# Hyena stage: a fourth weight unit is split ahead, in tiles of the common pool, from the stage's first unit on

## The chip, the cores and the metric

The program runs on one core of one Trainium2 chip. The metric is the device time of one execution in microseconds (us), lower is better; it is given as the median of several executions. TensorE (PE in the profile) multiplies matrices, VectorE (DVE) and ScalarE (ACT) do elementwise work, GpSimd (POOL) does a little of it, and SyncE (SP) issues the DMAs.

## The reference

The computation is a two-layer backbone over 256 latent tokens and 256 context tokens of width 1024. Layer 0 mixes tokens by differential attention, layer 1 by Hyena, a long convolution done through a discrete Fourier transform. Each layer is a stack of half-step SwiGLU, mixer, half-step SwiGLU, with modulation and LayerNorm around each. The change concerns only the Hyena mixer of layer 1, which runs on the latent tokens:

```
u = dwconv3(h @ w_in, conv_w) + conv_b          # w_in: 1024 x 3072
x0, x1, v = split(u, 3)
y = irfft(rfft(x1 * v, 2L) * rfft(filter, 2L))  # long convolution, both directions
return (x0 * (y + (x1 * v) * d_skip)) @ w_o     # w_o: 1024 x 1024
```

## The kernel before, in words

Everything is float32, and every matrix product is made of three float32r matmuls: the weight is split in a high part `wH` and a low part `wL`, the activations likewise, and the product of the two low parts is left out. So each weight must be loaded, rounded to its high part by ScalarE (line 238) and subtracted from the raw value by VectorE (line 239), before TensorE can use it.

**The weight stream.** The class `Stream` holds all weight units in the order of their use, each 128 x 2048 values (1 MB) in the Hyena stage. A unit is loaded by SyncE (line 259) into one of two `raw` buffers, and when there is room, it is split. Room means: fewer than `W_BUFS` = 3 units hold a pair of `wH`/`wL` tiles, or fewer than `extra` units hold tiles of the common pool. A unit split into `wH`/`wL` takes two pieces of 1024 columns; a unit split into the common pool takes four pieces of 512 columns, each with its own pair of tiles `xwH`/`xwL`. `spare(n)` sets `extra` and calls `pump()`, which loads and splits all that there is room for at that place of the program. `done(it)` gives a unit's room back and pumps again. When a split is issued, it is put `LATER` = 200 steps later in the scheduler's priority than its place in the program.

**The common pool.** `blk` has 49 tiles of 128 x 512 float32. Nearly all intermediate values live in it: activations, spectra, tables, products. A tile is taken when its first writer is scheduled and given back after its last reader. A scheduler that goes by priorities and a model of the times fixes the order of the instructions on each engine before the program runs; on the chip each engine works its own list in order.

**The Hyena stage.** It has three parts. First, twelve units of `w_in` (called u0 to u11 here) are multiplied by the function `ramp`: u0 to u7 give x1 and v, u8 to u11 give x0. Units u0 and u1 go in step for the first five of the eight steps over the width; from u2 on each unit is 48 matmuls, into the PSUM tile `pxv`. After unit n, `end(pp, n)` does the short convolution (`cv`, or `x0keep` from u8 on), the product x1*v (`pkeep`), and the transposes of the product of unit n-2 (`ptr`, then split into `pTh`/`pTl`). After units 6 and 10 (`SPECTRUM`), `end` also runs the forward transform of one half of the channels: 24 matmuls into `uf`, then in `product` 13 or 14 VectorE instructions that multiply by the filter's spectrum, ending at line 1364 or 1366. At unit 9 the tables of the inverse transform are loaded (line 1306) and split (`bih`/`bil`). Second, eight groups of twelve matmuls into `yt` do the inverse transform, and VectorE multiplies by x0 and splits the result (`oh`). Third, `Project` multiplies by the four units of `w_o` (who0 to who3).

In `ramp`, a unit's room is given back right after its matmuls, except after units 6 and 10. There the call of `done`, and with it the split that it issues, stands behind the last VectorE instruction of the spectrum's product on VectorE's list:

```
            if f in late:
                with tc.issue_after(end(pp, f).ins):
                    st.done(it)
            else:
                st.done(it)
                end(pp, f)
```

In the kernel before, `extra` is 0 from the feed-forward stages until the line `st.spare(1)` behind the second part (line 1423). So during the twelve units only three units are split or in use at a time: u0 to u2 are split when the stage begins, and the end of unit n lets unit n+3 be split. The end of u6, behind the spectrum's product, lets u9 be split; the end of u10 lets who1 be split. The unit who3 is the one that goes into the common pool, after the inverse transform's matmuls have been issued.

Of the kernel before, what the change touches and what calls it, by code (L numbers as in the profile page):

```python
# [310 lines left out]
def backbone(ctx, tc, A, out):  # L311
# [106 lines left out]
    st = Stream(nc, tc, rawp, rawap, wsp, blk, items, strict)  # L418
# [93 lines left out]
    def gemm(outs, X, nk, k0=0, k1=None):  # L512

        for k in range(k0, nk if k1 is None else k1):
            xh, xl = X[k]
            for o, w, opens in outs:
                h, lo = w(k)
                mm(o, h, xh, opens and k == 0, False)
                mm(o, h, xl, False, False)
                last = mm(o, lo, xh, False, k == nk - 1)  # L520
        return last
# [760 lines left out]
    def ramp(unit, gemm, X, end, n, late=(), first=2, ks=5):  # L1282


        grp = [unit() for _ in range(first)]
        gemm([o for g in grp for o in g[2]], X, KT, 0, ks)
        for f in range(n):
            if f < first:
                it, pp, outs = grp[f]
                gemm(outs, X, KT, ks)  # L1290
            else:
                it, pp, outs = unit()
                gemm(outs, X, KT)
# [6 lines that stand above are left out]
# [21 lines left out]
    def hyena(X, au):  # L1321
# [17 lines left out]
        def spectrum(dh):  # L1339
            pT = pTs.pop(dh)  # L1340
            U = {}
            for f in range(2):
                for ft in (f, 2 + f):
                    ps = bank("uf")
                    for tt in range(2):
                        c = slice(P * ft, P * ft + P)
                        h, lo = pT[tt]
                        mm(ps, au[tt][0][:, c], h, tt == 0, False)
                        mm(ps, au[tt][0][:, c], lo, False, False)
                        mm(ps, au[tt][1][:, c], h, False, tt == 1)  # L1350
                    U[ft] = ps
                last = product(f, dh, U[f], U[2 + f])
            return last
# [34 lines left out]
        def end(pp, n):  # L1388
# [15 lines left out]
            if n in SPECTRUM:  # L1404
                return spectrum(SPECTRUM.index(n))

        ramp(unit, gemm, [(x[:, :T], x[:, T:]) for x in X], end, 12, SPECTRUM)
        O = []
        for j in range(KT):
# [25 lines left out]
    norm = ffn("a", 1, X, lambda: (tables.extend(split_table(A["a_u"], "au")), spec_load(0)))  # L1435
    X = ln_apply(norm, ln_params(1, 0), 1, x256, R)
    norm = hyena(X, tables)
    X = ln_apply(norm, ln_params(1, 1), 1, x256, R)
    st.spare(0)
# [26 lines left out]
```

## Time and profile before

| | |
|---|---|
| median of 3 runs | 1352.83 us (1350.25 to 1353.7) |
| the profiled execution | 1354.76 us, span 1353.0 us |
| TensorE busy | 1305.6 us (96%) |
| VectorE busy | 1031.9 us (76%) |
| ScalarE busy | 666.5 us (49%) |
| mean granted TensorE clock | 0.975 |
| the Hyena stage's twelve units | from 1014.8 to 1107.6 us |

An execution outside the profile and the profiled one differ by about 2 us, of which the median run is the shorter. A row of the timeline gives the start in us, the duration, the engine, the line, the operation, what it writes and reads, and in brackets the idle time of that engine ahead of it with what ended it. Rows for PE show how long each matmul was in the array; matmuls overlap, so the distance from one start to the next is the rate. A row of the table by stretches gives for each engine the busy time in us and the number of instructions, then the granted TensorE clock as a share of full speed.

### The profile page before, as it was taken

To read this page: it belongs to the slowest core of one execution; us is meant where nothing else is said; L and a number is where in the kernel's file an instruction comes from. 1 tells how busy PE (TensorE), PEld (TensorE's weight loads), DVE (VectorE), ACT (ScalarE), POOL (GpSimd) and SP (SyncE) were. 2 spreads that over 40 slices of the span, in tenths; PEclk is the share of its full clock that TensorE was granted. 3 is DMA by queue.
4 is the path that set the end of the run, shared out by engine and by line. 5 is a ranking of instruction groups with operands and counts; after the bars stand their busy time and mean duration, and the time that the engine had idled before them with its cause. 6 is when DMAs were issued, how large, how long until landed. Compare 5 with 4: busy or idle time off the path is not lost.

```text
span 1353.0 us, 19211 instructions
## 1 busy us (share of the span) xinstructions
PE 1305.6 (96%) x7394; PEld 1126.5 (83%) x7394; DVE 1031.9 (76%) x1913; ACT 666.5 (49%) x1185; POOL 12.7 (1%) x12
## 2 busy tenths in 40 slices
PE   7999999999999999998999999999999899999997
PEld 5588888888888788887888888888889798888886
DVE  5699998889887777768767668766768889766664
ACT  3543222222223867656765446665446444755543
POOL 0000000000000000000000000000000110000000
PEclk8999999999998999998999998999999999999999
DMA  8777798888841212212554464554653435345452
GB/s 320 306 293 277 270 347 333 311 346 317 326 151 73 94 63 94 94 63 92 204 198 172 153 209 156 204 194 156 218 210 125 141 125 183 129 179 188 146 189 78
DMA packets 44386, 261.39 MB, mean 193 GB/s; under 512 B 4932, under 2 KB 6660, under 8 KB 19592
## 3 DMA queue, kind: packets, MB, share of 16 engines
q1 hardware_dynamic: 44296, 260.18, 52.9%
q8 instruction: 58, 0.95, 0.3%
q14 instruction: 32, 0.26, 0.1%
HBM read 257.01 MB, written 3.15 MB: 192 GB/s over the span
## 4 chain that ended last, share of the span: by engine, by line
PE 81%; DVE 9%; ACT 4%; DMA 3%; issue 1%; ACTq 0%; SPq 0%; DVEq 0%
PE pa L335 23%; PE pu L335 22%; PE py L335 19%; PE pxv L335 5%; DVE wL L239 3%; PE pv L335 2%; ACT wH L238 2%; DMA raw<-woa 1%; PE pka L335 1%; PE hsp L335 1%; PE pkb L335 1%; PE uf L335 1%; PE lnst L335 1%; PE po L335 1%; DMA raw<-wib 1%
## 5 line engine op out<-in xcount | busy, mean ns | idle before, releaser
L239 DVE TENSOR_TENSOR wL<-raw,wH 128x1024 fp32r<-128x1024 f32 (+1 forms) x356 | 387.9, 1108 | 121.2 <-ACT wH L238 118.9
L238 ACT CAST wH<-raw 128x1024 fp32r<-128x1024 f32 (+1 forms) x356 | 328.7, 955 | 207.0 <-PE py L335 94.4
L335 PE MATMUL pa<-xhl,wH 128*128 128x512 f32 x520 | 189.0, 400 | 5.6 <-DVE xhl L822 5.6
L335 PE MATMUL pu<-xhl,wH 128*128 128x512 f32 x520 | 188.3, 398 | 0.0
L335 PE MATMUL py<-g,wH 128*128 128x512 f32 (+1 forms) x594 | 185.8, 371 | 0.0
L491 DVE SCALAR_TENSOR_TENSOR rawa<-rawa,condb 128x1024 f32<-128x1024 f32 x128 | 151.6, 1219 | 5.9 <-DMA rawa<-adr 5.7
L335 PE MATMUL py<-g,wL 128*128 128x256 f32 x528 | 147.4, 279 | 0.0
L335 PE MATMUL pa<-xhl,wL 128*128 128x256 f32 x520 | 147.2, 283 | 0.0
L335 PE MATMUL pu<-xhl,wL 128*128 128x256 f32 x520 | 147.1, 283 | 0.0
L335 PEld LDWEIGHTS py<-g,wH 128*128 128x128 f32 x594 | 107.1, 188 | 20.5
L335 PEld LDWEIGHTS pa<-xhl,wH 128*128 128x128 f32 x520 | 99.0, 191 | 29.1 <-DVE xhl L822 4.2
L335 PEld LDWEIGHTS pu<-xhl,wH 128*128 128x128 f32 x520 | 98.9, 190 | 22.9
L335 PEld LDWEIGHTS pa<-xhl,wL 128*128 128x128 f32 x520 | 100.0, 192 | 0.1
L335 PEld LDWEIGHTS pu<-xhl,wL 128*128 128x128 f32 x520 | 99.7, 192 | 0.0
L335 PEld LDWEIGHTS py<-g,wL 128*128 128x128 f32 x528 | 99.6, 189 | 0.1
L852 ACT ACTIVATE sil<-pa 128x512 f32<-128x512 f32 x22 | 13.2, 599 | 146.9 <-PE pa L335 146.9
L335 PE MATMUL pxv<-xhl,wH 128*128 128x256 f32 x384 | 73.7, 293 | 1.1 <-ACT xhl L820 1.1
L335 PE MATMUL pa<-xh,wH 128*128 128x512 f32 x176 | 68.8, 391 | 0.0
L335 PE MATMUL pa<-xl,wH 128*128 128x512 f32 x176 | 68.6, 390 | 0.0
L335 PE MATMUL pu<-xh,wL 128*128 128x512 f32 x176 | 68.6, 390 | 0.0
L335 PE MATMUL pu<-xl,wH 128*128 128x512 f32 x176 | 68.5, 389 | 0.0
L335 PE MATMUL pa<-xh,wL 128*128 128x512 f32 x176 | 68.5, 389 | 0.0
(315 smaller groups left out, 2593.9 us busy)
## 6 DMA issues: line engine op xcount, KB each, us to landing
rawa<-adr SPq DMA_DIRECT2D x64, 1024.0 KB, 6.9
raw<-wia SPq DMA_DIRECT2D x44, 1024.0 KB, 4.8
raw<-wib SPq DMA_DIRECT2D x44, 1024.0 KB, 4.7
raw<-woa SPq DMA_DIRECT2D x32, 704.0 KB, 4.3
raw<-wob SPq DMA_DIRECT2D x32, 704.0 KB, 4.1
rawa<-adx SPq DMA_DIRECT2D x8, 1024.0 KB, 9.6
raw<-wqk SPq DMA_DIRECT2D x8, 1024.0 KB, 4.7
raw<-whv SPq DMA_DIRECT2D x8, 1024.0 KB, 4.8
```

Source lines behind the costliest of these rows:

```text
L238: nc.scalar.copy(h[:, d], it["raw"][:, s:e])
L239: nc.vector.tensor_tensor(lo[:, d], it["raw"][:, s:e], h[:, d].bitcast(F32), OP.subtract)
L335: return nc.tensor.matmul(o, l, r, start=start, stop=stop, skip_group_check=True)
L491: V.scalar_tensor_tensor(junk if q else w, w, 1.0, condb[:, q, :], OP.mult, OP.mult, accum_out=mod[i][:, q, 2 * u + h:2 * u + h + 1])
L852: S.activation(s, pa, AF.Silu)
```

## The change

One line is added in `hyena`, ahead of the call of `ramp`:

```
             if n in SPECTRUM:
                 return spectrum(SPECTRUM.index(n))
 
+        st.spare(1)
         ramp(unit, gemm, [(x[:, :T], x[:, T:]) for x in X], end, 12, SPECTRUM)
         O = []
         for j in range(KT):
```

From here on one more unit may be split, into tiles of the common pool. With u0, u1 and u2 in the three `wH`/`wL` slots, u3 goes into the pool at once. After that, the end of unit n lets unit n+4 be split, and it takes the kind of tiles that unit n had: u3, u7, u11 and who3 stand in the pool, all others in `wH`/`wL`. The end of u6 now lets u10 be split, the end of u10 lets who2 be split. The later `st.spare(1)` finds nothing left to do. No matmul, no transform and no load is added or taken away; three units (u3, u7, u11) are split in four pieces of 512 columns where there were two of 1024.

More of the change, by code (lines that the diff above doesn't have):

```diff
@@ L1405, in end @@
                 return spectrum(SPECTRUM.index(n))
+        st.spare(1)
         ramp(unit, gemm, [(x[:, :T], x[:, T:]) for x in X], end, 12, SPECTRUM)
```

## Prediction

> **What bounds the kernel now.** I read the page first. TensorE is busy nearly all the time, and the chain that ended last is mostly its matmuls, so only time in which TensorE waits or runs at a lower clock can be won.
>
> ```profile
> span 1353.0 us, 19211 instructions
> ...
> PE 1305.6 (96%) x7394; PEld 1126.5 (83%) x7394; DVE 1031.9 (76%) x1913; ACT 666.5 (49%) x1185; POOL 12.7 (1%) x12
> ...
> PE 81%; DVE 9%; ACT 4%; DMA 3%; issue 1%; ACTq 0%; SPq 0%; DVEq 0%
> ```
>
> The change acts on one stage, so the table by stretches comes next: from unit u7 to the second transform, in steps of 10 us.
>
> ```profile
> core 0: us, PE busy (x) PEld busy (x) DVE busy (x) ACT busy (x) POOL busy (x), PEclk, DMA share, GB/s
> 1060.00:1070.00 10.00, 10.00 (x70) 9.34 (x69) 6.29 (x13) 3.74 (x7) 0.00 (x0) 1.00 0.40 152
> 1070.00:1080.00 10.00, 6.78 (x55) 6.37 (x53) 8.50 (x16) 5.66 (x12) 6.53 (x4) 1.00 0.18 54
> 1080.00:1090.00 10.00, 7.29 (x40) 6.83 (x41) 7.62 (x14) 3.38 (x7) 0.00 (x0) 0.66 0.40 135
> 1090.00:1100.00 10.00, 10.00 (x73) 9.43 (x72) 8.42 (x13) 6.96 (x10) 0.00 (x0) 1.00 0.75 284
> ```
>
> There is one hole: between 1070 and 1090 TensorE is idle for 20 - 6.78 - 7.29 = 5.93 us, and its clock falls to 0.66. Who ends the waits is in PE's timeline, and the lengths of the work in the chain.
>
> ```profile
> 1075.55 0.38 PE L1383 MATMUL ptr<-ident,pkeep 128*128 128x128 f32 x2
> 1075.69 0.48 PE L335 MATMUL pxv<-xhl,wH 128*128 128x256 f32 x2
> 1078.85 0.38 PE L335 MATMUL pxv<-xhl,wL 128*128 128x256 f32 x1 [2.69 <-DVE wL L239]
> 1082.71 0.69 PE L1383 MATMUL ptr<-ident,pkeep 128*128 128x128 f32 x2 [3.24 <-DVE pkeep L1397]
> 1084.78 0.41 PE L335 MATMUL pxv<-xhl,wL 128*128 128x256 f32 x1
> ...
> 1107.45 0.28 PE L335 MATMUL yt<-bih,yh 128*128 128x256 f32 x1
> ```
> ```profile
> 1058.54 5.46 PE uf L335 x24
> ...
> 1101.86 5.75 PE pxv L335 x48
> ```
>
> At 1075.69 TensorE begins u9 and lacks its low part: the first half comes at 1078.85, the second lets the unit go on at 1084.78. From 1075.69 to the first `yt` matmul at 1107.45 are 31.76 us. The work in it is three units of 5.75 (u9, u10, u11) and one transform of 5.46, 22.7 us together. So **9.0 us are lost there**: 5.9 idle, the rest by the clock.
>
> Why u9 is late is on VectorE's and ScalarE's lists.
>
> ```profile
> 1056.87 1.21 DVE L239 TENSOR_TENSOR wL<-raw,wH 128x1024 fp32r<-128x1024 f32 x1
> ...
> 1062.60 0.48 DVE L1328 SCALAR_TENSOR_TENSOR cv<-pxv,vec,cv 128x255 f32<-128x255 f32 x1 [3.15 <-ACT cv L1327]
> ...
> 1066.44 0.68 DVE L1359 TENSOR_TENSOR yr<-uf,spec 128x512 f32<-128x512 f32 x1
> ...
> 1075.90 0.69 DVE L1364 TENSOR_TENSOR yi<-yi,yt 128x512 f32<-128x512 f32 x1
> ...
> 1076.71 2.09 DVE L239 TENSOR_TENSOR wL<-raw,wH 128x1024 fp32r<-128x1024 f32 x1
> ...
> 1082.24 0.42 DVE L1397 TENSOR_TENSOR pkeep<-cv 128x256 f32<-128x256 f32 x1
> ...
> 1083.17 1.22 DVE L239 TENSOR_TENSOR wL<-raw,wH 128x1024 fp32r<-128x1024 f32 x1
> 1084.51 1.22 DVE L239 TENSOR_TENSOR wL<-raw,wH 128x1024 fp32r<-128x1024 f32 x1
> 1086.44 1.22 DVE L239 TENSOR_TENSOR wL<-raw,wH 128x1024 fp32r<-128x1024 f32 x1
> 1090.27 2.36 DVE L239 TENSOR_TENSOR wL<-raw,wH 128x1024 fp32r<-128x1024 f32 x2 [2.61 <-ACT wH L238]
> ```
> ```profile
> 1060.11 2.00 ACT L238 CAST wH<-raw 128x1024 fp32r<-128x1024 f32 x2 [2.56 <-DMA raw<-wh]
> ```
>
> ScalarE makes u9's high part at 1060.11, but its low part stands on VectorE behind the spectrum's product (1066.44 to 1076.59), as `ramp` orders for the unit that u6 makes room for. The four single pieces from 1076.71 on are u9's halves, then u10's; the pair at 1090.27 is u11.
>
> **The change part by part.** *u9 leaves the place behind the product.* It is now let in by the end of u5. Half a unit's high part takes 1.0 us and its low part 1.2, and VectorE had 3.15 us idle ahead of 1062.60. Its load had landed by 1060.11 (the wait ahead of that row is for it) and now can only come earlier, and u5's slot is free long before. So u9 is split before the product and TensorE runs it from 1075.69 to 1081.44. This removes the whole wait at u9; price on VectorE nothing, since 2.4 us fall in its 3.15 us gap. Without that cover the product would begin up to 2.4 us later.
>
> *u10 takes its place.* Now u10 stands behind the product. I let its halves take u9's old places: the first ends at 1078.80, the second at 1084.39. The first half is there when TensorE arrives at 1081.44; the second isn't, and since the two halves of a unit are used in turn at each step, TensorE waits until 1084.39: 2.95 us. The transposes of `pkeep` from 1082.24 lie within that wait. At best, the halves follow each other and end at 1079.9; then only the transposes wait, for about 1.2 us from 1081.44 to 1082.67. At worst, VectorE isn't a bit faster and the second half stays where u10's was, ending at 1087.66: 6.2 us.
>
> *The clock.* The stretches of 3.4 us around this hole and around another one show how the clock reacts:
>
> ```profile
> 582.40:585.80 3.40, 1.72 (x13) 1.32 (x13) 3.40 (x12) 2.82 (x6) 0.00 (x0) 1.00 0.55 234
> 585.80:589.20 3.40, 3.40 (x18) 3.40 (x17) 3.40 (x8) 2.81 (x7) 0.00 (x0) 0.50 0.02 5
> ...
> 1077.30:1080.80 3.50, 0.62 (x3) 0.41 (x3) 3.46 (x7) 1.88 (x5) 2.64 (x2) 0.99 0.00 0
> 1080.80:1084.20 3.40, 1.49 (x5) 1.27 (x6) 3.40 (x7) 1.00 (x3) 0.00 (x0) 0.50 0.00 0
> 1084.20:1087.60 3.40, 3.40 (x16) 3.16 (x16) 3.40 (x6) 0.78 (x2) 0.00 (x0) 0.50 0.59 207
> ```
>
> After a stretch with TensorE half idle (1.72 of 3.40 us busy) the next one has half the clock and 1.7 us of it are lost. At the present hole two stretches are slow, in which 1.49 + 3.40 us of matmuls run at half rate: 2.4 us lost. A wait of 2.95 us should still cost one slow stretch, 1.7 us. The Trainium skill (TensorE: Matmul & The Clock Gate, The HAM clock gate) says that the clock falls after at least one idle window of about 3.4 us. By that rule the new wait would leave the clock alone and the gain would be 1.7 us larger; the rows at 582.40 speak against it, where half a window was enough.
>
> *Sum at the matmuls.* The loss of 9.0 us becomes 2.95 + 1.7 = 4.65 us: **4.35 us gained**. With the second half at its best place it becomes 1.2 us, a gain of 7.8; with the worst one 6.2 + 2.4, a gain of 0.4.
>
> *The four-piece splits.* u3, u7 and u11 are split in four pieces:
>
> ```profile
> L238 ACT CAST xwH<-raw x8: 603/612/622, 1126.3 to 1164.9; 128x512 fp32r<-128x512 f32 x8
> L239 DVE TENSOR_TENSOR xwL<-raw,xwH x8: 678/692/693, 1126.9 to 1166.2; 128x512 fp32r<-128x512 f32 x8
> ```
> ```profile
> L239 DVE TENSOR_TENSOR wL<-raw,wH x14: 1207/1218/2114, 1054.7 to 1124.2; 128x1024 fp32r<-128x1024 f32 x14
> ```
>
> Four times 0.692 is 2.77 us on VectorE against 2.44, and 2.45 on ScalarE against about 2.1: 0.35 us more on each, three times. For u3 and u7 it is hidden, since from u1 to u7 TensorE doesn't wait; the first and the last of these stretches, all four full:
>
> ```profile
> 1020.00:1030.00 10.00, 10.00 (x86) 10.00 (x85) 7.99 (x17) 8.07 (x14) 0.00 (x0) 1.00 0.25 85
> ...
> 1050.00:1060.00 10.00, 10.00 (x80) 9.71 (x79) 8.97 (x17) 4.17 (x8) 0.00 (x0) 1.00 0.72 263
> ```
>
> u11's is behind u10's and ahead of its use by about 2 us or more (VectorE reaches it by about 1088, TensorE at about 1097). If uncovered it costs 0.35.
>
> *The DMAs.* No load is added; all come earlier. u11's load now follows u9's split instead of waiting for it until 1084.4, so the 2.61 us that VectorE waited for u11 go. SP's list also holds the loads of the second spectrum and of the tables; they stay between the same units, and the tables are needed only at 1107.
>
> *What is late next.* Behind the matmuls stands VectorE's work for the second product and for `oh`:
>
> ```profile
> 1098.73 0.68 DVE L1359 TENSOR_TENSOR yr<-uf,spec 128x512 f32<-128x512 f32 x1
> ...
> 1107.60 0.69 DVE L1364 TENSOR_TENSOR yi<-yi,yt 128x512 f32<-128x512 f32 x1
> ...
> 1125.36 0.41 DVE L510 TENSOR_TENSOR oh<-pkeep,oh 128x256 fp32r<-128x256 f32 x1
> ```
>
> It must move forward by the same 4.35 us, or the gain is lost at `oh`. Ahead of it VectorE has u9's pieces less (2.09 + 1.22 = 3.3), 0.35 more for u11, and 2.61 of idle time less to wait for: room for 5.6 us. who1's split moves ahead of the second product, who2 takes its place behind it. So I count nothing lost here, and nothing gained. Later stages see the same stream, with who3 in the pool in both kernels.
>
> So the profiled execution's 1354.76 us (span 1353.0 and 1.76 around it) would become 1350.4, and the median of 1352.83, which lies 1.9 below the profiled one, **1348.5**.
>
> **The rivals.** *The hole closes (gain 6 to 8, 1345 to 1347).* VectorE puts u10's halves close together, or the clock stays up. For it: with u9 gone, `pkeep` and u10 are all that is urgent behind the product. Against it: 1076.71 to 1084.39 also holds the convolutions of u7 and u8, which the order before put between the two halves. By the skill's rule on the clock, above, the time would be 1352.8 - 6.05 = 1346.8.
>
> *The gain is eaten on VectorE (gain 0 to 2, about 1352).* u10's halves stay where they are, or u11's pieces are put ahead of them. The same list of VectorE work then ends at the same time and TensorE only waits at u10 instead of u9. By the bound above the gain is 0.4. Against it: 3.3 us of work really leave the stretch.
>
> *The pool runs out (slower).* The place is u11's split. Counted from the code, at about 1092 the pool holds 43 of its 49 tiles: 4 of the residual, 8 inputs, 4 tables and 4 transposes of the forward transform, 4 `pkeep`, 5 of the spectrum, 8 products, 4 tables of the inverse, 2 `x0keep`. u11's eight make 51. Two low pieces would have to wait until the second transform's last matmul gives back eight tiles. If VectorE takes them up at once, that costs about 1.4 us. If they come behind the second product, which runs from 1098.73 to 1108.29, 9.6 us, of which 3.1 lie ahead of the transform's end at 1101.86, TensorE waits 6.4 + 1.4 = 7.8 us at u11 and 2.4 for the clock: 10.2, so 1352.8 - 4.35 + 10.2 = 1358.7. It decides the sign as soon as more than 4.35 us of that product stand ahead of the last piece. Against it: the split's place in the priorities, 200 steps behind u7, is just ahead of that product.
>
> *It does nothing* would need that the room isn't used; but u3 is loaded at that time and goes in at once, so I give it no chance of its own.
>
> **How the numbers follow.** I give the main case 0.55, with a range of its own from 1346.8 to 1350.3; the closed hole 0.18; the gain eaten 0.15; the pool 0.12. A measurement of this kernel tells about 0.3% (4.1 us) from no change, so faster means below 1348.8. The main case lies across that line, a little more than half below it: 0.32 faster, 0.23 same. With the closed hole, faster is 0.50; with the eaten gain, same is 0.38; slower 0.12. The range from 1344.5 to 1354.0 takes in the first three cases and leaves out most of the pool's.
>
> **What would show it.** Right: no wait for `wL` at u9; one shorter wait for u10's second half near 1081 to 1084; the first `yt` matmul near 1103; xwH and xwL counted 34 where there are 22 now; u9's low part ahead of 1066. Wrong: TensorE's hole as long as before but at u10 (eaten); a wait for xwL ahead of u11, behind line 1364 or 1366 (pool); `oh` still ending near 1125 with TensorE waiting for it; or a new wait between 1025 and 1069, where there was none.

## The result, and the profile after

The changed kernel takes 1364.75 us in the median of five executions (1360.75 to 1367.79), the kernel before 1353.65 (1350.25 to 1355.59) beside it. A sixth execution, disturbed at 7244 us, is left out; with it the median is 1365.01, the figure that later expectations go by. The ratio on record is 1.0097, with a 95% interval from 1.0075 to 1.0118; the two medians differ by 0.8%, and a repetition (e16) gives 1.0100. So the change makes the kernel **slower by about 1%**, 11 to 12 us, outside the predicted range of 1344.5 to 1354.0. The profiled execution took 1364.75 us, with a span of 1363.0 against 1353.0.

On the first page nearly nothing changes: TensorE's busy time, the shares of the chain.

```profile
span 1363.0 us, 19224 instructions
...
PE 1308.0 (96%) x7394; PEld 1128.2 (83%) x7394; DVE 1034.0 (76%) x1919; ACT 667.0 (49%) x1191; POOL 13.3 (1%) x12
...
PE 81%; DVE 9%; ACT 4%; DMA 3%; issue 2%; POOL 0%; POOLq 0%; ACTq 0%; SPq 0%; DVEq 0%
```

The stage must be read in stretches, with the columns of the table shown of before.

```profile
1050.00:1060.00 10.00, 7.11 (x47) 7.12 (x48) 8.96 (x17) 4.45 (x9) 0.00 (x0) 0.83 0.73 274
...
1080.00:1090.00 10.00, 6.11 (x44) 5.90 (x44) 9.76 (x19) 6.67 (x12) 0.03 (x1) 0.90 0.66 236
1090.00:1100.00 10.00, 10.00 (x62) 9.20 (x61) 3.31 (x5) 3.39 (x5) 0.00 (x0) 0.93 0.66 238
...
1110.00:1120.00 10.00, 7.26 (x54) 6.46 (x54) 9.71 (x14) 4.55 (x9) 4.78 (x3) 1.00 0.01 2
1120.00:1130.00 10.00, 5.39 (x34) 5.19 (x33) 9.85 (x23) 2.33 (x7) 0.00 (x0) 0.78 0.51 197
```

Where before had one hole in TensorE's row, there are now three: 2.89 us idle in 1050 to 1060, 3.89 in 1080 to 1090, 2.74 + 4.61 = 7.35 in 1110 to 1130. And VectorE works only 3.31 us in the stretch from 1090, where in before it worked 8.42. What TensorE waited for in the whole stage:

```profile
PE ptr L1383 <- DVE pkeep L1397: 6.9, 2, 3.9
PE py L335 <- DVE oh L510: 4.6, 1, 4.6
PE yt L335 <- POOL yl L1370: 2.1, 2, 1.5
```

The wait for `wL` at u9 is gone, as predicted. In its place stand two waits for a `pkeep`, and at the end one for `oh`.

```profile
1052.89 0.44 PE L1383 MATMUL ptr<-ident,pkeep 128*128 128x128 f32 x2 [3.03 <-DVE pkeep L1397]
...
1087.83 0.53 PE L1383 MATMUL ptr<-ident,pkeep 128*128 128x128 f32 x2 [3.89 <-DVE pkeep L1397]
```

To compare runs, each point of the stage is counted from its first matmul of u0 (1014.78 in before, 1012.67 in after; all rows are TensorE's starts):

| us after the stage's start | before | after |
|---|---|---|
| first transform | 43.5 | 47.9 |
| inverse transform (`yt`) | 92.7 | 93.9 |
| Projection (`py`) | 104.2 | 109.2 |
| next stage (`pa`) | 136.9 | 148.0 |

The stage is 11.15 us longer, which is the whole loss: 1.24 up to `yt`, where 4.35 had been forecast as a gain, 3.79 from there to `py`, 6.12 in the Projection. Each run has one profile. The profile of e16, the same changed kernel, has 94.0, 109.3 and 150.1 us in the last three rows, so a difference of about 2 us between the stages of two profiles shows nothing.

The first two holes are read on VectorE's list.

```profile
1045.70 2.50 DVE L239 TENSOR_TENSOR xwL<-raw,xwH 128x512 fp32r<-128x512 f32 x4 [0.34 <-ACT xwH L238]
1048.12 0.87 DVE L1328 SCALAR_TENSOR_TENSOR cv<-pxv,vec,cv 128x255 f32<-128x255 f32 x2
1048.90 0.86 DVE L1329 SCALAR_TENSOR_TENSOR cv<-pxv,vec,cv 128x255 f32<-128x255 f32 x2
1049.68 1.21 DVE L239 TENSOR_TENSOR wL<-raw,wH 128x1024 fp32r<-128x1024 f32 x1
...
1052.41 0.75 DVE L1397 TENSOR_TENSOR pkeep<-cv 128x256 f32<-128x256 f32 x2
...
1076.55 4.56 DVE L239 TENSOR_TENSOR wL<-raw,wH 128x1024 fp32r<-128x1024 f32 x2
...
1081.23 1.28 DVE L239 TENSOR_TENSOR xwL<-raw,xwH 128x512 fp32r<-128x512 f32 x2
...
1082.64 1.28 DVE L239 TENSOR_TENSOR xwL<-raw,xwH 128x512 fp32r<-128x512 f32 x2
1083.84 0.47 DVE L1328 SCALAR_TENSOR_TENSOR cv<-pxv,vec,cv 128x255 f32<-128x255 f32 x1
...
1087.36 0.42 DVE L1397 TENSOR_TENSOR pkeep<-cv 128x256 f32<-128x256 f32 x1
1087.69 1.22 DVE L239 TENSOR_TENSOR wL<-raw,wH 128x1024 fp32r<-128x1024 f32 x1
...
1092.10 1.22 DVE L239 TENSOR_TENSOR wL<-raw,wH 128x1024 fp32r<-128x1024 f32 x1
1100.77 0.69 DVE L510 TENSOR_TENSOR bil<-tabf,bih 128x512 fp32r<-128x512 f32 x1 [7.46 <-ACT bih L509]
...
1102.95 0.68 DVE L1359 TENSOR_TENSOR yr<-uf,spec 128x512 f32<-128x512 f32 x1
```

u7's four pieces stand ahead of the convolutions of u3 and u4, a half of u8's between them and the `pkeep` that TensorE's transposes wait for: the first hole. In before u7's first half stood behind u3's `pkeep`:

```profile
1049.54 0.41 DVE L1397 TENSOR_TENSOR pkeep<-cv 128x256 f32<-128x256 f32 x1
...
1050.46 1.21 DVE L239 TENSOR_TENSOR wL<-raw,wH 128x1024 fp32r<-128x1024 f32 x1
```

u10's and u11's pieces stand ahead of u7's convolution: the second hole. Then comes the sight that matters most: at 1092.10 + 1.22 VectorE stops for **7.46 us**, for the second half of a table of the inverse transform (`bih`), and the second product, which stands behind it on the list, begins at 1102.95 in place of 1098.73 (90.3 us after the stage's start in place of 84.0). On ScalarE and SyncE that table looks so:

```profile
1100.12 0.62 ACT L509 CAST bih<-tabf 128x512 fp32r<-128x512 f32 x1 [2.69 <-PE uf L335]
```
```profile
1081.17 3.10 SPq L259 DMA_DIRECT2D raw<-who  x2
1084.33 0.43 SPq L1306 DMA_DIRECT2D tabf<-b_i  x1
1090.32 3.35 SPq L259 DMA_DIRECT2D raw<-who  x2
1093.72 0.42 SPq L1306 DMA_DIRECT2D tabf<-b_i  x1
```

ScalarE has the release of its output tile from a matmul of the second transform, so the pool was full: this wait, of 2.69 us, is the one that ended last. Ahead of the cast on ScalarE's list stands a pair of who's high parts, done at 1097.4. And the table's second load is issued only at 1093.72, behind four loads of the Projection's weights. In before both table loads were issued from 1070.27 on, ahead of all of those, and VectorE didn't stop ahead of the second half:

```profile
1070.27 4.53 SPq L1306 DMA_DIRECT2D tabf<-b_i  x2
...
1087.69 34.14 SPq L259 DMA_DIRECT2D raw<-who  x4
```
```profile
1085.85 0.68 DVE L510 TENSOR_TENSOR bil<-tabf,bih 128x512 fp32r<-128x512 f32 x1
```

### The profile page after: what moved, and what is told of

It is laid out like the page before. It is cut to its first block, busy times and chain, and to the rows that moved or that the text cites. A ratio compares the mean times of both kernels' runs of the same rounds, so it can differ in the third digit from the quotient of the medians.

```text
span 1363.0 us, 19224 instructions
## 1 busy us (share of the span) xinstructions
PE 1308.0 (96%) x7394; PEld 1128.2 (83%) x7394; DVE 1034.0 (76%) x1919; ACT 667.0 (49%) x1191; POOL 13.3 (1%) x12
## 4 chain that ended last, share of the span: by engine, by line
PE 81%; DVE 9%; ACT 4%; DMA 3%; issue 2%; POOL 0%; POOLq 0%; ACTq 0%; SPq 0%; DVEq 0%
PE pa L335 23%; PE pu L335 22%; PE py L335 20%; PE pxv L335 4%; DVE wL L239 3%; PE pv L335 2%; DMA raw<-woa 2%; ACT wH L238 1%; PE hsp L335 1%; PE pka L335 1%; PE pkb L335 1%; PE uf L335 1%; PE lnst L335 1%; PE po L335 1%; PE sc L1061 1%
## 5 line engine op out<-in xcount | busy, mean ns | idle before, releaser
L239 DVE TENSOR_TENSOR wL<-raw,wH 128x1024 fp32r<-128x1024 f32 (+1 forms) x350 | 381.4, 1108 | 115.2 <-ACT wH L238 113.0
L238 ACT CAST wH<-raw 128x1024 fp32r<-128x1024 f32 (+1 forms) x350 | 322.5, 954 | 210.8 <-PE py L335 98.3
L335 PE MATMUL pu<-xh,wH 128*128 128x512 f32 x176 | 68.5, 389 | 0.0
```

The costliest lines, as they stand in the source:

```text
L238: nc.scalar.copy(h[:, d], it["raw"][:, s:e])
L239: nc.vector.tensor_tensor(lo[:, d], it["raw"][:, s:e], h[:, d].bitcast(F32), OP.subtract)
L335: return nc.tensor.matmul(o, l, r, start=start, stop=stop, skip_group_check=True)
```

## The experiments

Three theories stood against each other. **P**: the pool is full, so `bih` waits for a tile. **Q**: the order of the lists; splits stand ahead of convolutions whose `pkeep` TensorE needs. **R**: in the Projection, who3's pieces stand ahead of `oh`. A fourth, **S** (the place of the table's load on SyncE's list), was added after e5. "Stage" is the time from u0's first matmul to the next stage's first. Each ratio is to runs of the kernel before on the same chip; times of different chips are best compared by these ratios.

**e1, the tables asked for later** (the changed kernel):

```diff
-TABLE_LOAD = 9
+TABLE_LOAD = 11
```

> The changed kernel with the inverse transform's tables loaded and split after unit u11 instead of after u9 (TABLE_LOAD 11). Theory P (the pool is full: u11's eight tiles leave no tile for the table's high part bih, which waits for the second forward transform, and VectorE stands 7.5 us behind it): the 7.5 us of idle time on VectorE ahead of bil go, the second product begins right behind the second transform, and the time falls by about 4 to 8 us from 1365, to 1357 to 1361; not the whole, since the tables' own load and split now come later. Theory Q (the loss is the order of the lists: splits stand ahead of the convolutions, and TensorE waits for pkeep): the two waits for pkeep of 3.0 and 3.9 us stay, and the time stays within 2 us of 1365.

1368.94 us, ratio 1.0124 (1.0097 to 1.0152): not faster. VectorE's idle time ahead of the second product went, and that product ran from 84.7 us after the stage's start, as in before (84.0). But on SyncE's list the table's loads now stood behind the next stage's weights, and TensorE waited for the table itself:

```profile
PE yt L335 <- ACT bih L509: 14.5, 1, 14.5
```

So the miss says nothing against P. It is the first sign that a load's place on SyncE's list counts.

**e2, u11 not in the pool** (the changed kernel; the room is taken back at the end of u6, so u3 and u7 alone stand in the pool):

```diff
+            if n == 6:
+                st.spare(0)
             if n == SPEC_LOAD:
```

> The changed kernel with the room taken back after u6's transform (spare(0) in end(6)), so that u3 and u7 are split into the pool, u11 is not, and from u11 on the stream is that of before. Theory P: the pool never fills, VectorE's idle time of 7.5 us and the late second product go, and the time comes back to 1353 or less (1347 to 1354). Theory Q: the wait for pkeep near 1052 of 3.0 us and its slow clock stay, the second one shrinks since u11's pieces no longer stand ahead of the convolution of u7; 1358 to 1362.

1350.16 us, ratio 0.9978 (0.9961 to 0.9996), 1.2% less than the change by the ratios. So the whole loss goes when u11 stays out of the pool. This run doesn't tell how: it relieves the pool, and it also gives u11 and the Projection's weights their old places, so that the table's second load stands behind one of them in place of four (issued 69.4 us after the stage's start) and the second hole shrinks to 1.1 us. The first hole is still there:

```profile
1056.96 0.44 PE L1383 MATMUL ptr<-ident,pkeep 128*128 128x128 f32 x2 [3.26 <-DVE pkeep L1399]
```

**e3, the kernel before with eight tiles of the pool held** from the stage's start to u11's end; eight small writes and reads are added:

```diff
+        held = [blk("held") for _ in range(8)]
+        for t in held:
+            V.memset(t[:, 0:8], 0.0)
...
+            if n == 11:
+                for t in held:
+                    nc.gpsimd.tensor_tensor(t[:, 0:8], t[:, 0:8], X0[5][:, 0:8], OP.add)
```

> The kernel before with eight tiles of the pool taken at the start of the Hyena stage and given back only after the convolution of u10; the stream and its splits are those of before. Eight tiny instructions on VectorE and eight on GpSimd are added for it. Theory P: the pool fills as in the changed kernel, bih waits for the second transform, VectorE idles some 5 to 8 us there, and the time is 6 to 11 us over before: 1359 to 1364. Theory Q: nothing is ahead of the convolutions, so the time stays within 2 us of 1353.5.

1356.87 us, ratio 1.0035 (1.0018 to 1.0053). Nothing of the weight stream is changed here, and yet VectorE stops ahead of `bil`:

```profile
1097.31 0.69 DVE L510 TENSOR_TENSOR bil<-tabf,bih 128x512 fp32r<-128x512 f32 x1 [6.66 <-ACT bih L509]
```

A full pool alone makes that stop. As in the change, ScalarE's list has a pair of who's high parts ahead of `bih` (done at 1094.4), and the last 2.25 us are for the tile, released by a matmul of the second transform. It costs about 4.5 us (2.4 to 7.2 by the interval), less than the 6 to 11 that P expected.

**e4, the kernel before with u9's split no longer behind the product:**

```diff
-        ramp(unit, gemm, [(x[:, :T], x[:, T:]) for x in X], end, 12, SPECTRUM)
+        ramp(unit, gemm, [(x[:, :T], x[:, T:]) for x in X], end, 12, SPECTRUM[1:])
```

> The kernel before without the order that puts the split after u6 behind the first product (only the one after u10 stays). If the hole at u9 is made by that order, as the prediction had it: u9 and u10 are split ahead of the product, TensorE's hole of 9.0 us shrinks to 1 to 3 us, and the time falls by 5 to 9 us to 1344 to 1349. If the hole is made by the load on VectorE as a whole (the same work has to be done before pkeep of u7): TensorE waits for pkeep instead, and the time stays within 3 us of 1353.5.

1355.88 us, ratio 1.0025 (1.0008 to 1.0043): no gain, though u9 was early and the wait for `wL` gone. The next unit's halves stood ahead of the product, and the first waited for a slot that u7 still held, and TensorE waited 3.8 and 4.4 us for what lay behind:

```profile
1070.25 1.22 DVE L239 TENSOR_TENSOR wL<-raw,wH 128x1024 fp32r<-128x1024 f32 x1 [6.06 <-ACT wH L238]
```

**e5, e6, e7: more tiles, and its controls.** A pool of 53 fits if the attention's weights have two raw buffers in place of three. e5 is the changed kernel with both, e6 the changed kernel and e7 the one before with two raw buffers alone.

```diff
-RAWA_BUFS = 3
-BLK_BUFS = 49
+RAWA_BUFS = 2
+BLK_BUFS = 53
```

> The changed kernel with 53 tiles in the common pool in place of 49; the room comes from the attention weights' raw buffers, two in place of three. In the stage the engines' lists are the same as in the changed kernel with two raw buffers and 49 tiles (e6), so that only the number of tiles differs. Count at the fullest point by the lists: 51 tiles. Theory P (pool full): VectorE's idle 7.46 us ahead of bil goes to under 1 us, the second product begins at 93 to 96 us after the stage's start in place of 90.3 to 104, the stage (first unit's matmul to the next stage's first) falls by 6 to 9 us against e6 and the total by as much. Theory Q (the splits' place in the lists is the whole loss): the stage falls by under 2 us, since the lists are the same. By either the two waits of TensorE's transposes for pkeep (3.0 and 3.9 us) and py's wait for oh (4.6 us) stay, so that the stage stays 3 to 6 us longer than the one of before.

> Control: the changed kernel with two raw buffers for attention weights and the pool of 49. All theories: the stage as in the changed kernel (135 us, within 2), the idle 7.5 us ahead of bil there; the total moves only by what the attention and the other stages lose to the missing buffer, 0 to 8 us.

> Control: the kernel before with two raw buffers for attention weights and the pool of 49. All theories: the stage as before (122 us, within 2); the total moves by the same 0 to 8 us as in e6, so that e6 less e7 is 11 to 13 us, as after less before.

| | time, us | ratio | stage, us |
|---|---|---|---|
| e7, before, 49 tiles | 1364.13 | 1.0100 (1.0074 to 1.0125) | 136.1 |
| e6, after, 49 tiles | 1377.01 | 1.0190 (1.0161 to 1.0220) | 149.8 |
| e5, after, 53 tiles | 1376.23 | 1.0181 (1.0151 to 1.0211) | 150.1 |

The missing buffer costs about 13 us in both (by the ratios), more than the 8 expected, and e6 less e7 is 12.9, about the change's own loss. The expectations put the stage at 135 and 122 us; by the measure used here it is 148.0 us in the change and 136.9 in before, and the controls lie within 2 us of that. But **P as put falls**: with four tiles more, nothing is won. In e5 the wait has another end:

```profile
1114.44 0.62 ACT L509 CAST bih<-tabf 128x512 fp32r<-128x512 f32 x1 [1.62 <-DMA tabf<-b_i]
```

The table's second load was issued at 1109.12, again behind four loads of the Projection. In both runs the cast of `bih`'s second half begins about 88 us after the stage's start (87.8 in e6, 88.5 in e5), held once by the tile and once by the load. Two causes end at nearly the same time, and taking one away shows nothing.

**e8, one unit in the pool for a short while** (the kernel before, with `st.spare(1)` at the end of u4 and `st.spare(0)` at that of u5):

> The kernel before, with room for one more unit in the pool only from the end of unit 4 to the end of unit 5: u8 alone is split into pool tiles, u3, u7 and u11 keep their slots. By the lists u9's split then stands ahead of u4's convolution and u10's behind the product. Theory P alone (nothing but the full pool cost time): the prediction's gain at the matmuls comes, 2 to 4 us, 1348 to 1351. Theory Q (a split put into the list ahead of a convolution holds the pkeep that a transpose waits for): the wait for wL at u9 goes and one for pkeep comes in its place in front of u5 to u7, 2 to 4 us; the total within 2 us of before, 1351 to 1355.

1351.81 us, ratio 1.0005 (0.9986 to 1.0025). The wait for `wL` is gone and one of 4.4 us for a `pkeep` has come, as Q expects.

```profile
1065.35 0.69 PE L1383 MATMUL ptr<-ident,pkeep 128*128 128x128 f32 x2 [4.42 <-DVE pkeep L1401]
```

**e9 and e10: the table's loads on a queue of their own**, with 49 and with 53 tiles (two raw buffers as in e5 to e7):

```diff
-            nc.sync.dma_start(t, src[:, 512 * h:512 * h + 512])
+            (nc.gpsimd if name == "bi" else nc.sync).dma_start(t, src[:, 512 * h:512 * h + 512])
```

> The changed kernel as in e6 (two raw buffers, 49 tiles), the inverse table's two loads issued from GpSimd's queue in place of SyncE's, where the second stands behind four loads of the Projection's weights. Only the queue is relieved; the pool is still full. Theory P (the full pool is what ends the wait, e5's 53 tiles having run into the table's load only 1.3 us short of it): bih's second cast still waits for the second transform, bil's idle 5 to 8.6 us on VectorE, total within 4 us of e6. Theory S (the load's place on SyncE's list is the whole cause): bil's idle under 1 us, total 6 to 9 us less than e6.

> The same with 53 tiles: queue and pool both relieved. Theory PS (two causes that end within 1.5 us of each other, so that taking away one alone, as in e5, brings nothing): bil's idle under 1 us, the second product begins at 91 to 96 us after the stage's start, the stage falls by 6 to 9 us against e5 and e6 and the total with it, 1367 to 1371, 3 to 7 above e7. Theory P as first put (e5 should have cured it) and a theory that neither matters: within 2 us of e5, 1374 to 1378.

| stage, us (time, us) | 49 tiles | 53 tiles |
|---|---|---|
| SyncE's queue | 149.8 (1377.01) | 150.1 (1376.23) |
| GpSimd's queue | 147.7 (1376.53) | **137.2 (1364.02)** |

Either mended alone gives nothing in the time; both together give 12.5 us (e9 to e10, on one chip), more than was expected, and by the ratios (e10 1.0104, e7 1.0100) that is the whole loss against e7. In e9 the load itself had to wait for a tile on GpSimd's queue:

```profile
1103.12 0.54 POOL L1306 DMA_DIRECT2D tabf<-b_i  x1 [10.34 <-DVE pTl L510]
```

It landed within 3.1 us, at about 1106, yet `bih`'s second half began only at 1112.39. On ScalarE's list it stands behind a pair of who's high parts, and those waited for who's load:

```profile
1110.49 2.00 ACT L238 CAST wH<-raw 128x1024 fp32r<-128x1024 f32 x2 [5.84 <-DMA raw<-who]
1112.39 0.61 ACT L509 CAST bih<-tabf 128x512 fp32r<-128x512 f32 x1
```

So what ended last in e9 is this place on the list, not a tile. In e10 `bih` stands ahead of that pair. VectorE waits 1.67 us at the first half and none at the second, and the second product begins 85.5 us after the stage's start, where e5 had 91.4:

```profile
1093.57 1.23 POOL L1306 DMA_DIRECT2D tabf<-b_i  x2
```
```profile
1103.05 0.69 DVE L510 TENSOR_TENSOR bil<-tabf,bih 128x512 fp32r<-128x512 f32 x1 [1.67 <-ACT bih L509]
...
1107.26 0.68 DVE L510 TENSOR_TENSOR bil<-tabf,bih 128x512 fp32r<-128x512 f32 x1
```

With P and S mended TensorE's wait for `oh` falls from 4.6 to 1.0 us, though who3's four pieces still stand ahead of VectorE's work for `oh`:

```profile
PE ptr L1383 <- DVE pkeep L1397: 7.0, 2, 3.9
...
PE py L335 <- DVE oh L510: 1.0, 1, 1.0
```

So R needs no cause of its own: most of that wait follows from the late second product. The two waits for `pkeep` are untouched. One reserve is needed: the scheduler knows how many tiles there are, so e10's lists differ from e9's. Besides the place of `bih`, each `bil` stands one of who's low parts further ahead on VectorE, and in the Projection who3's pieces alternate with the work on `pkeep`, where in e9 they follow each other. So the two by two shows that tiles and queue must both be relieved. How much of the 12.5 us the free tiles bring by themselves, and how much by the order that the scheduler makes of them, isn't separated. e5 and e6 have the same lists in the stage.

**e11 and e12: the order mended.** e11 is e2, e12 a kernel like e8, with the splits that units 3 and 4 make room for put behind those units' `pkeep`:

```diff
-                V.tensor_tensor(Pk[n], cv[:, :T], cv[:, T:], OP.mult)
+                last = V.tensor_tensor(Pk[n], cv[:, :T], cv[:, T:], OP.mult)
...
+            return last
...
-        ramp(unit, gemm, [(x[:, :T], x[:, T:]) for x in X], end, 12, SPECTRUM)
+        ramp(unit, gemm, [(x[:, :T], x[:, T:]) for x in X], end, 12, list(SPECTRUM) + [3,4])
```

> e2 (u11 not in the pool) with the room that units 3 and 4 leave given to the next splits only behind their convolutions (the list of VectorE then has cv3, cv4 and their pkeep ahead of the splits of u7 and u8). Theory Q (a split in the list ahead of a convolution holds the pkeep of a transpose): the wait of 3.26 us for pkeep near 40 us goes or falls under 1 us, and 2 to 4 us of e2's time with it: 1346 to 1349, ratio 0.995 to 0.998. A rival, that VectorE is simply behind by then and the wait moves to a later pkeep or wL: 1349 to 1352, with a new wait of 2 to 4 us between 45 and 75 us.

> e8 (room for one unit only from the end of unit 4 to that of unit 5) with the same order behind units 3 and 4, so that u7 is the unit in the pool. Theory Q: e8's wait of 4.4 us for pkeep goes, 1346 to 1349. Rival (VectorE behind, the wait moves on): 1349 to 1353.

**e11 takes 1344.31 us, ratio 0.9950 (0.9925 to 0.9974)**, faster than both kernels. Its stage is 129.4 us, in e2 134.2. Of TensorE's waits for a `pkeep` or a `wL` one of 1.4 us is left:

```profile
PE ptr L1383 <- DVE pkeep L1400: 1.4, 1, 1.4
```

e12 takes 1349.24, ratio 0.9989 (0.9973 to 1.0006): the hole of e8 went and one of 3.8 us for u7's `pkeep` came, the rival's expectation.

**e13, e14, e15.** e13 is e10 with e11's order, so that P, S and Q are all mended with the change intact. e14 is the changed kernel with that order alone. e15 keeps SyncE's queue and 53 tiles, with `TABLE_LOAD = 6`.

> e10 (the changed kernel, two raw buffers, 53 tiles, the table's loads on GpSimd's queue) with units 3 and 4's room given to the next splits only behind their convolutions, as in e11. If the three causes add: the wait for pkeep near 40 us after the stage's start goes, and 4 to 7 us of e10's time: 1357 to 1360, 4 to 7 below e7 (1364.1), which is the gain that was predicted for the change. If the wait only moves: 1362 to 1366.

> The changed kernel itself (three raw buffers, 49 tiles, SyncE's queue) with only that order mended. The full pool and the table's load stay, so bil still idles 5 to 9 us on VectorE; the wait for pkeep near 40 us (3.0 us and its clock) goes, the second (3.9 us, behind u10's and u11's pieces) stays: 1359 to 1362, between the change (1365.0) and before (1353.7). If the order carried the whole loss: 1350 to 1354; if nothing: 1363 to 1367.

> The changed kernel with two raw buffers and 53 tiles, the table loaded on SyncE's queue as before, but asked for at unit 6 in place of unit 9, ahead of all four loads of the Projection's weights. If the place on the queue is what counts: as e10, 1362 to 1366, bil without an idle of over 1 us. If GpSimd's queue as such made e10 faster: 1372 to 1378 as e5.

e14: 1358.73 us, just under what was expected, ratio 1.0062 (1.0041 to 1.0084), with a stage of 144.3 against the change's 148.0; `bil` still stops VectorE for 7.83 us. e13: 1360.30 us, ratio 1.0076 (1.0044 to 1.0109), with a stage of 133.9 us against 137.2 in e10 and 136.1 in e7. The times of e13 lie 3.7 and 3.8 us below those two, but on another chip and with intervals that overlap, and the stages are of one profile each, so whether the three causes add isn't settled. The first hole is gone in e13; the second one stays:

```profile
1093.07 0.69 PE L1383 MATMUL ptr<-ident,pkeep 128*128 128x128 f32 x2 [4.40 <-DVE pkeep L1398]
```

e15: 1370.38 us, ratio 1.0138 (1.0098 to 1.0179), between the two cases expected. The second product isn't held up any more, and the stage (141.5) is 8.6 below e5's, but the table's pieces now stand ahead of u6's convolution and weren't loaded by then. All that lies behind them on VectorE's list came later, and TensorE waited 7.2 us for u7's `pkeep`, where e5 had 3.9:

```profile
1082.33 1.33 DVE L510 TENSOR_TENSOR bil<-tabf,bih 128x512 fp32r<-128x512 f32 x2 [7.55 <-ACT bih L509]
```

It supports S, but doesn't settle how much of e10's gain is the queue's own.

**e16, e17, e18: the order's share on one chip.** The change, e14 and e11 once more, side by side.

> The changed kernel as it is, beside e17 and e18 on one chip: ratio to before 1.0075 to 1.012, as in the result.

> e14 on the same chip as e16. If the order carries about a third of the loss, as the stages of the traces say (144.3 against 148.0 us): 3 to 5 us below e16. If over half, as the medians of two chips say: 6 to 7.

> e11 on the same chip: ratio to before 0.993 to 0.9975, by the stage's 7.5 us less than before's in the trace near 0.9945.

The change takes 1364.07 us, ratio 1.0100 (1.0083 to 1.0117); with the order mended 1359.94, 1.0059 (1.0039 to 1.0079); with u11 out of the pool as well 1345.33, 0.9959 (0.9944 to 0.9975). So the order alone carries 4.1 us of the loss, about a third, and the slowest execution of e17 (1361.05) lies below the fastest of e16 (1362.88). This and the 12.5 us of the table come to more than the loss, since the wait at u9, which the change removes, is part of the balance. The gain of e11 is there again.

## Why the prediction was wrong, step by step

**u9 leaves the place behind the product: right.** Its low part was ahead of the product, and TensorE didn't wait for a `wL` any more.

**u10 takes its place: wrong in the cause, and too small.** Forecast was a wait of 2.95 us (1.2 to 6.2) for u10's second half; it was 3.89, for u7's `pkeep`. u10's halves were both there at 1081.11, before TensorE was through with u9 at 1083.94. The prediction left that `pkeep` at its old time (1082.24) in every case. But u10's halves took 4.56 us together, and u11's pieces, which it put behind and out of the way, stood ahead of u7's convolution too (2.56 us), so that it came at 1087.36.

**"For u3 and u7 it is hidden, since from u1 to u7 TensorE doesn't wait": wrong.** This step counted only the 0.35 us by which four pieces are longer. What it left out is where they stand: a whole split came forward by one unit on VectorE's list, ahead of two convolutions. That cost 3.03 us of waiting and in this execution a slow stretch of the clock (0.83 over 1050 to 1060). e16 and e17 show it: with the same splits behind the convolutions the time falls by 4.1 us, and the first hole is gone.

**"they stay between the same units, and the tables are needed only at 1107": wrong, and with the full pool the costliest step** (12.5 us, e9 to e10). The tables' loads did stay between the same units, but the loads of the Projection moved ahead by one unit, past them, and each waits for a raw buffer. "All come earlier" fails here: the second load of the table went out 81 us after the stage's start in place of 60.0. And 1107 is when TensorE needs the table; VectorE needs it about 9 us earlier, since `bil` stands ahead of the second product on its list.

**The pool's rival: right in its count, wrong in its victim.** Forecast were 51 tiles for 49 places, with two of u11's pieces waiting behind the product. The pool was full, but u11's pieces got theirs first, and the table's tile was what waited last, in front of the whole product and not inside it. At 0.12 it was too unlikely. At 1358.7 it was too cheap: it had no term for the splits ahead of the convolutions (4.1 us in e17), nor for the work behind `yt`. And it left out the load, which ends at the same time, so that free tiles alone would not have helped.

**"So I count nothing lost here": wrong.** VectorE's tail came 9.4 us later (the product's last line 1364 at 102.2 us after the stage's start, 92.8 in before), and 9.91 us of the loss lie behind `yt`.

**The clock: right by the row in the profiled execution, but no fixed price.** Holes of 3.03 and 3.89 us each brought a slow stretch (0.83 over ten microseconds is one stretch of 3.4 at half the clock). Other profiles of the same lists differ: in e6 the first hole (3.02 us) brought none, with the clock at 1.00 over the 20 us around it, and in e5 (2.99 us) it brought two (0.66 over 1065.94 to 1075.94). So the 1.7 us that the prediction counts for such a hole can be 0 to 3.4. The hole of 1.4 us in e11 brought none:

```profile
1068.37:1078.37 10.00, 8.59 (x73) 8.39 (x71) 9.95 (x17) 7.24 (x13) 3.38 (x2) 1.00 0.36 131
```

The Trainium skill (TensorE: Matmul & The Clock Gate, The HAM clock gate) speaks of at least one idle window of about 3.4 us before the clock falls; here the hole of 3.03 us, shorter than that, was enough.

What the sum at the matmuls is worth when the rest is mended stays open. e13 reaches `yt` 1.9 us earlier than its control e7 (90.0 against 91.9 us after the stage's start), with the second hole still there, where 4.35 had been forecast; that is about what two profiles with the same lists differ by there (94.2 in e6, 96.0 in e5). e11, which keeps u11 out of the pool and has no hole over 1.4 us, is another kernel: it takes 1344.3 and, in e18, 1345.3 us, by the ratios 0.4 to 0.5% less than before, about the gain that the prediction gave to the closed hole.

## What to carry to other kernels

When work is let in earlier, follow every list that it is moved past to the instruction that now stands behind it: the loads on the issuing engine as well as the pieces on VectorE, and ask of each what it waits for and who stands in line behind it. If lifting one limit changes nothing, look for a second one that ends at the same moment, and lift both in a two-by-two test with controls. Extra buffering should be taken back before the stage's fullest point, and splits of later weights put behind the work that the matrix engine waits for next.

## What the runs showed of the hardware

Two `wL` pieces of VectorE took 4.56 us at 1076.55, where one took 1.22 at 1087.69; GpSimd was computing `yl` at that time:

```profile
1075.97 1.83 POOL L1370 TENSOR_TENSOR yl<-yr,yh 128x512 fp32r<-128x512 f32 x1 [1.55 <-ACT yh L1369]
1077.75 2.28 POOL L1370 TENSOR_TENSOR yl<-yi,yh 128x512 fp32r<-128x512 f32 x1
...
1107.78 1.29 POOL L1370 TENSOR_TENSOR yl<-yr,yh 128x512 fp32r<-128x512 f32 x1 [27.75 <-ACT yh L1369]
```

The second `yl` took 2.28 us too, where the one at 1107.78 took 1.29. The Trainium skill (GPSIMD Engine Reference, 1. Specifications) says that GpSimd shares its way to the memory with VectorE and contends with VectorE's instructions that have two inputs there, which these have; the rows agree. Two `yl` of 1.29 and two pieces of 1.22 add up to 5.0 us, and from 1075.97 to 1081.11 the four took 5.1, as if they went one after the other; that is an estimate from these rows, and no run here moves `yl` away to test it. The two pieces put right behind the product cost 4.56 us in place of 2.44.

An issue that waits for a buffer held the later issues of its engine. In e5, with tiles to spare, the table's second load (256 KB) went out 83.2 us after the stage's start, in before by 60.0, right behind the weight loads that wait for a raw buffer, which the table doesn't use. In e10, with the same tiles but on GpSimd's queue, both loads went out from 67.6 us on.

```profile
1105.72 3.35 SPq L259 DMA_DIRECT2D raw<-who  x2
1109.12 0.42 SPq L1306 DMA_DIRECT2D tabf<-b_i  x1
```

The Trainium skill (DMA: Bandwidth & Descriptors, Issuing engines are not separate DMA queues) says that issuing from several engines saves only the issuing time, usually little beside the transfer. No run here tests that for bandwidth. But the time that it saved the table was that of the waits ahead of it on the list, and with the tiles to match it was worth 12.2 us (e10 against e5, on two chips; by the ratios, 1.0104 against 1.0181, about 10).
